# Weight preparation in three stages: load, square, and sum with scale, each a few steps apart

## The chip, the cores and the metric

The kernel runs on one core of one Trainium2 chip. The metric is the device time of the program in microseconds (us), measured in three runs. One further execution was profiled; all rows below come from it. The engines are TensorE (PE, matrix products; PEld is its weight load), VectorE (DVE), ScalarE (ACT), GpSimd (POOL) and SyncE (SP), which issues the loads.

## The reference

One decoder layer in float32 on 512 tokens of width 2048:

```python
hn = rms_norm(h, norm_mix)
h = h + nsa_mixer(hn, nsa_w_in, nsa_w_out, ...)      # sparse attention, 16 heads, 4 groups
hn = rms_norm(h, norm_ffn)
h = h + jnp.square(jax.nn.relu(hn @ ffn_w1)) @ ffn_w2    # F = 8192
gate = jax.nn.sigmoid(rms_norm(h, norm_ple) @ ple_w_gate)
h = h + (p @ ple_w_proj) * gate
return rms_norm(h, norm_final)
```

## The kernel before

The attention comes first (0 to about 870 us), then the MLP (to about 2110 us), then the gate stage. What follows speaks of the weights of the last two, since the change lies there.

**A weight's way.** A product in float32 accuracy is made of three matmuls on float16 halves: weight high x data high, weight high x data low, weight low x data high. So each weight goes through these steps, in pieces ("quarters") of 128 x 1024 float32, 512 KB:

1. *load* into one of six raw buffers (`raw`, RAWS = 6), issued by SP (L702);
2. *square*: ACT squares it and adds along each partition (`sum_sq`, L677; the squares themselves go to a PSUM bank and are not used, the trace calls them `s_ps`), which leaves one number per partition, `sq4`;
3. *sum*: PE adds these over the partitions with 128x1 matmuls against a tile of ones, `wb` (`scale_of`, the trace's `s_ps<-sq,wb`); a pair of weights has four such matmuls, a single one two;
4. *scale*: three small DVE operations make a power of two of the sum (L670 to L672);
5. *split*: ACT writes the scaled high half `wh` (L683), DVE the low half `wl` (L684), into one of nine slots (SLOTS = 9). The raw buffer is free once its last split is done.

**Items and the G loop.** The hidden width 8192 is worked in 16 groups G of four blocks. A group has `up` (h @ w1) and `down` (@ w2). From G = 2 on, `up` takes two "pair" items: two weight blocks of two quarters each, which `prepare` turns into seven slots, four of them with sums and differences of quarters (`S1`, `S2`, `s3`, `s4`, DVE adds at L725 to L731), for a scheme with seven products of 24 matmuls of 128x256 in place of eight. `down` takes four items of two quarters, 48 matmuls of 128x512 each. One G takes some 81 us, and the loop runs `down(G)`, then `up(G + 2)`.

**What orders the preparation.** `pump` (L751) does as much preparation as the buffers allow each time it is called: after every slot that is used up (`used`), and after three of the four steps `e` of a `down` item. At one call, in this order: scales of items that were staged at least LAG = 2 calls ago, loads and squares (`stage`) while raw buffers are free, splits while slots are free. At the attention's end `early` stages and scales the first five items one by one, with a lag of 0. The order in which a program's instructions then stand on each engine is settled by a scheduler that lists them by times of its own; each engine works strictly in that order.

Names that come up below: `x_ps` tiles are PSUM banks (`pt_ps` and `g_ps` hold products), `fh` and `fl` the halves of the hidden values, `xch` and `xcl` those of the MLP's input, `z` a copy of a product that is needed twice (L984), `ft` the hidden values before their square (L948), `fq` their sums of squares.

Of the kernel before, what the change touches and what calls it, by code (L numbers as in the profile page):

```python
# [9 lines left out]
BF16 = mybir.dt.bfloat16  # L10
# [16 lines left out]
NG = F // 128 // FG  # L27
NB = 32
HOLD = 9
LAG = 2  # L30
RAWS = 6
SLOTS = 9
STD = 2
# [8 lines left out]
def trunk_kernel(ctx, tc, xT, pT, gains, w_kcvc, w_blk, w_gates, w_out, w1c, w2c, posT,  # L42
# [21 lines left out]
    def sbank():  # L64
        return ps.tile([128, 2 * S], F32, name="s_ps", tag="s2", bufs=1)
# [18 lines left out]
    P = {}  # L84
# [23 lines left out]
    def wslice(hs, off, n=128):  # L108
# [31 lines left out]
                       fill=0.0, base=0, channel_multiplier=-1)  # L140
# [331 lines left out]
    def merge(gens, nfill, fill):  # L472
        n = [0] * len(gens)
        total = sum(c for _, c in gens)
        done = 0
        order = sorted((((j + 0.5) / c, gi) for gi, (_, c) in enumerate(gens) for j in range(c)))
        for x, (_, gi) in enumerate(order):
            next(gens[gi][0], None)
            want = int((x + 1) * nfill / total)
            while done < want:  # L480
                next(fill, None)
                done += 1
        for gg, _ in gens:
            drain(gg)
        while done < nfill:
            next(fill, None)
            done += 1

    with tc.tile_pool(name="st", bufs=2) as st:
# [3 lines left out]
        for c in range(2):  # L493
# [5 lines left out]
            for u in range(4):  # L499
                if c == 0:  # L500
                    n = 4 if u == 0 else 2
# [173 lines left out]
    def sum_sq(junk, src, sq):  # L675
        with nc.allow_low_precision(reason="a power of two is taken from it"):
            ACT.activation(junk, src, AF.Square, accum_out=sq)  # L677
# [15 lines left out]
    def stage(it):  # L693
        it.raw = []
        if len(it.src) == 2:
            quarters = [(it.src[a], b) for a, b in ((0, 0), (1, 0), (1, 1), (0, 1))]
        else:
            quarters = [(it.src[0], b) for b in range(need(it))]
        ps4 = P["sm"].tile([128, 4], BF16, name="sq4", tag="sq4")
        for x, (src, b) in enumerate(quarters):  # L700
            r = P["raw"].tile([128, 1024], F32, name="raw", tag="raw")
            nc.sync.dma_start(out=r, in_=src[:, b * 1024:(b + 1) * 1024])  # L702
            sum_sq(sbank()[:, 0:1024], r, ps4[:, x:x + 1])
            it.raw.append(r)
        it.sq = ps4[:, 0:len(quarters)]
        it.at = st["pumps"]

    def slot(it, name, src):
        hi = P["w16"].tile([128, 1024], F16, name="wh", tag="wh")
# [33 lines left out]
        if G > 0:  # L743
            items += [Item(ffn2[G - 1, c]) for c in range(4)]
    items += [Item(pT), Item(w_proj[1])] + [Item(w_pg[m]) for m in range(NK)]
    st = {"staged": 0, "split": 0, "gen": None, "raws": 0, "slots": 0, "limit": 0, "taken": 0, "scaled": 0, "pumps": 0}

    def need(it):
        return it.src[0].shape[-1] // 1024 * len(it.src)

    def pump(lag=LAG):  # L751
        st["pumps"] += 1
        while True:
            n = st["scaled"]
            if n < st["staged"] and st["pumps"] - items[n].at >= lag:
                items[n].sc, items[n].inv = scale_of(items[n].sq)
                st["scaled"] += 1
                continue
            n = st["staged"]
            if n < min(len(items), st["limit"]) and st["raws"] + need(items[n]) <= RAWS:  # L760
                stage(items[n])
                st["raws"] += need(items[n])
                st["staged"] += 1
                continue
            n = st["split"]
            if n < st["scaled"] and st["slots"] < SLOTS:
                if st["gen"] is None:
                    st["gen"] = prepare(items[n])
                    st["left"] = 7 if need(items[n]) == 4 else need(items[n])
                next(st["gen"])  # L770
                st["slots"] += 1
                st["left"] -= 1
                if need(items[n]) == 4:
                    st["raws"] -= {2: 2, 1: 1, 0: 1}.get(st["left"], 0)
                else:
                    st["raws"] -= 1
                if st["left"] == 0:
                    next(st["gen"], None)
                    st["gen"] = None
                    st["split"] += 1  # L780
                continue
            return
# [4 lines left out]

    def take():
        st["taken"] += 1
        return items[st["taken"] - 1]  # L790

    def early(n0, n1, gains=False):
        if gains:
            gain_scales()
            yield
        for n in range(n0, n1):
            st["limit"] = n + 1
            pump(0)
            yield

    def gain_scales():
# [16 lines left out]
    for hd in range(HEADS):  # L818
        n = counts[hd]
        pvg = pv_stage(hd, (pp, opool))  # L820
        if hd == 0:
            merge([(pvg, 10)], 16, fill)
            merge([(s_stage(1, (pp, small)), 5)], n - 16, fill)
        elif hd % HPG == 3 and hd + 1 < HEADS:
            merge([(pvg, 10)], 40, fill)
            merge([(s_stage(hd + 1, (pp, small)), 5)], n - 40, fill)
        elif hd + 2 < HEADS:
            merge([(pvg, 10), (s_stage(hd + 1, (pp, small)), 5)], n, fill)
        elif hd + 1 < HEADS:
            merge([(pvg, 10), (s_stage(hd + 1, (pp, small)), 5), (early(0, 2, True), 3)], n, fill)  # L830
        else:
            merge([(pvg, 10), (early(2, 4), 2)], n, fill)
        if hd == HEADS - 3:
            x_sb.close()
            for nm, bufs in (("sm", 12), ("keepc", 1), ("w16", SLOTS), ("raw", RAWS)):
                P[nm] = pool(nm, bufs)
        if hd == HEADS - 2:
            lo_eng[0] = DVE
    merge([(early(4, 5), 2)], 16, fill)
    drain(fill)  # L840
    a_sb.close()
    P["S"] = pool("S", 2, side="left")
# [66 lines left out]
    with ExitStack() as fx:  # L909
# [55 lines left out]
        def up_pair(G, j0, fq, ts, hook):  # L965
            it = take()
            ninv = P["sm"].tile([128, 1], F32, name="ninv", tag="ninv")
            DVE.tensor_scalar(ninv, it.inv, -1.0, None, op0=OP.mult)
            z = {}
            c = [wk.tile([128, S], F32, name="ft", tag="t") for _ in range(2)]  # L970
            o = {}

            def prod(b, w, x, first):
                if first:
                    o[b] = gbank()
                wh, wl = it.w[w]
                for k in range(8):
                    ws = slice(k * 128, (k + 1) * 128)
                    xh, xl = X[x, k]
                    mm3(o[b][:, 0:H2], wh[:, ws], wl[:, ws], xh, xl, first and k == 0, k == 7)  # L980

            def keep(n):
                z[n] = wk.tile([128, H2], F32, name="z", tag="z")
                ACT.activation(z[n], o["x"][:, 0:H2], AF.Copy)  # L984

            def total(e, half, n, b):
                DVE.tensor_add(c[e][:, half * H2:(half + 1) * H2], z[n], o[b][:, 0:H2])  # L987

            prod("x", "11", "11", True)
            keep(1)  # L990
            used()
            prod("v", "12", "21", True)
            total(0, 0, 1, "v")
            used()
            prod("x", "S2", "t2", False)
            keep(2)
            used()
            prod("y", "S1", "t1", True)
            used()
            hook(G, j0)  # L1000
            prod("x", "s3", "T3", False)
            keep(3)
            total(1, 1, 3, "y")
            used()
            prod("u", "22", "T4", True)
            total(1, 0, 3, "u")
            used()
            prod("y", "s4", "22", False)
            total(0, 1, 2, "y")
            used()  # L1010
            for e in (1, 0):
                DVE.tensor_scalar(c[e], c[e], ninv if e else it.inv, 0.0, op0=OP.mult, op1=OP.max)
            for e in range(2):
                squares(c[e], fq, j0 + e, ts)

        def up(G, prev=None):
            fq = P["sm"].tile([128, FG], F32, name="fq", tag="fq")
            ts = []

            def hook(G, j0):  # L1020
                if prev and j0 == 0:
                    sqd.append(squash(*prev))
                if G == 0 and j0 >= 2:
                    combos(j0 - 2)
                if G == 1 and j0 < 3:
                    combos(2 + 2 * j0)
                    combos(3 + 2 * j0)

            if G < STD:
                up_std(G, fq, ts, hook)  # L1030
            else:
                for j0 in (0, 2):
                    up_pair(G, j0, fq, ts, hook)
            return ts, fq

        def squash(ts, fq):
# [40 lines left out]
        for G in range(NG):  # L1077
            if G == NG - 1:
                st["limit"] = len(items) - NK + 2
            down(*sqd[G], G == NG - 1, made if G + 1 < NG else None)  # L1080
            if G + 2 < NG:
                made = up(G + 2)
# [154 lines left out]
```

## Time and profile before

| what | value |
|---|---|
| median of 3 runs | 2376.61 us (2374.44 to 2377.46) |
| profiled execution | 2376.99 us, span 2375.3 us |
| PE busy | 2315.4 us, 97% of the span |
| DVE, ACT, POOL busy | 1569.4, 1288.8 and 327.3 us |
| granted TensorE clock | 0.995 |
| moved by DMA | 232.52 MB, 98 GB/s in the mean |

The span reaches from the first to the last instruction; the execution's own time is 1.7 us longer. A matmul is drawn until its modelled end, which lies behind the start of the next, so the row of a wait shows less than what was lost; the times from start to start tell it.

### The profile page before, as it was taken

To read this page: it belongs to the slowest core of one execution; us is meant where nothing else is said; L and a number is where in the kernel's file an instruction comes from. 1 tells how busy PE (TensorE), PEld (TensorE's weight loads), DVE (VectorE), ACT (ScalarE), POOL (GpSimd) and SP (SyncE) were. 2 spreads that over 40 slices of the span, in tenths; PEclk is the share of its full clock that TensorE was granted. 3 is DMA by queue.
4 is the path that set the end of the run, shared out by engine and by line. 5 is a ranking of instruction groups with operands and counts; after the bars stand their busy time and mean duration, and the time that the engine had idled before them with its cause. 6 is when DMAs were issued, how large, how long until landed. Compare 5 with 4: busy or idle time off the path is not lost.

```text
span 2375.3 us, 35243 instructions
## 1 busy us (share of the span) xinstructions
PE 2315.4 (97%) x14042; PEld 1644.1 (69%) x14042; DVE 1569.4 (66%) x2737; ACT 1288.8 (54%) x2125; POOL 327.3 (14%) x176
## 2 busy tenths in 40 slices
PE   8999999999999999999999999999999999999997
PEld 6888888888888778567656665765576567654445
DVE  6347646656656968876776677667767776665742
ACT  5324434334333668576556656655665566565951
POOL 4253232333333120000000000000000000002012
PEclk9999999999999999999999999999999999999999
DMA  5231122122122413233223323332333233242411
GB/s 197 97 111 67 66 78 71 67 76 72 71 72 96 143 51 129 73 114 116 90 88 121 120 83 104 109 115 88 116 107 100 88 124 116 89 156 67 133 63 72
DMA packets 59062, 232.52 MB, mean 98 GB/s; under 512 B 6928, under 2 KB 7312, under 8 KB 51728
## 3 DMA queue, kind: packets, MB, share of 16 engines
q1 hardware_dynamic: 58896, 230.25, 28.9%
q8 instruction: 110, 1.80, 0.3%
q14 instruction: 56, 0.46, 0.1%
HBM read 223.94 MB, written 6.29 MB: 97 GB/s over the span
## 4 chain that ended last, share of the span: by engine, by line
PE 71%; DMA 10%; ACT 8%; DVE 6%; issue 4%; POOL 0%; SPq 0%; ACTq 0%; DVEq 0%; POOLq 0%
PE g_ps L71 42%; PE pt_ps L71 20%; DMA raw<-in_ffn_dram 9%; PE s_ps L71 5%; ACT wh L683 4%; ACT s_ps L677 3%; PE o_ps L71 3%; DVE wl L684 2%; PE pt_ps L427 1%; DVE ft L987 1%; DVE S L729 0%; DVE xt L881 0%; PE pt_ps L419 0%; DVE p L384 0%; DVE h L299 0%
## 5 line engine op out<-in xcount | busy, mean ns | idle before, releaser
L71 PEld LDWEIGHTS <-wh 128*128 128x128 f16 x6336 | 612.3, 98 | 353.0 <-issue 25.1
L684 DVE SCALAR_TENSOR_TENSOR wl<-raw,sc,wh 128x1024 f16<-128x1024 f32 x266 | 342.3, 1290 | 229.9 <-ACT wh L683 225.4
L71 PEld LDWEIGHTS <-wl 128*128 128x128 f16 x3168 | 309.7, 98 | 192.3 <-issue 24.7
L677 ACT ACTIVATE s_ps<-raw 128x1024 f32<-128x1024 f32 x294 | 301.1, 1024 | 239.8 <-DMA raw<-in_ffn_dram 206.5
L683 ACT ACTIVATE wh<-raw,sc 128x1024 f16<-128x1024 f32 x266 | 300.8, 1138 | 74.4 <-PE g_ps L71 61.2
L80 POOL TENSOR_TENSOR wl<-raw,wh 128x1024 fp32r<-128x1024 f32 x100 | 241.5, 2420 | 507.5 <-ACT wh L79 480.4
L179 POOL TENSOR_TENSOR ssacc<-ssacc,sq 128x512 f32<-128x512 f32 x50 | 71.3, 1427 | 1468.6 <-issue 1328.0
L79 ACT ACTIVATE wh<-raw 128x1024 fp32r<-128x1024 f32 (+1 forms) x122 | 125.6, 1044 | 225.0 <-PE g_ps L71 157.8
L71 PE MATMUL g_ps<-ah,wh 128*128 128x512 f32 x544 | 215.2, 396 | 0.0
L71 PE MATMUL g_ps<-ah,wl 128*128 128x512 f32 x544 | 214.1, 394 | 0.0
L71 PE MATMUL g_ps<-al,wh 128*128 128x512 f32 x544 | 212.7, 391 | 0.0
L71 PE MATMUL pt_ps<-fh,wh 128*128 128x512 f16 (+1 forms) x544 | 202.9, 373 | 3.5 <-ACT z L984 3.5
L71 PE MATMUL pt_ps<-fl,wh 128*128 128x512 f16 (+1 forms) x544 | 202.9, 373 | 0.0
L71 PE MATMUL pt_ps<-fh,wl 128*128 128x512 f16 (+1 forms) x544 | 202.9, 373 | 0.0
L71 PE MATMUL g_ps<-fh,wh 128*128 128x512 f16 (+1 forms) x544 | 202.8, 373 | 0.0
L71 PE MATMUL g_ps<-fh,wl 128*128 128x512 f16 (+1 forms) x544 | 202.7, 373 | 0.0
L71 PE MATMUL g_ps<-fl,wh 128*128 128x512 f16 (+1 forms) x544 | 202.7, 373 | 0.0
L684 DVE SCALAR_TENSOR_TENSOR wl<-S,sc,wh 128x1024 f16<-128x1024 f32 x112 | 143.5, 1281 | 88.0 <-ACT wh L683 88.0
L683 ACT ACTIVATE wh<-S,sc 128x1024 f16<-128x1024 f32 x112 | 128.0, 1142 | 69.9 <-PE pt_ps L71 42.1
L377 ACT ACTIVATE p<-s_ps,nm 128x128 f32<-128x128 f32 (+3 forms) x128 | 66.3, 524 | 113.9 <-DVE scm L373 57.3
L71 PE MATMUL pt_ps<-xcl,wh 128*128 128x256 f16 x448 | 122.1, 273 | 0.0
L71 PE MATMUL pt_ps<-xch,wh 128*128 128x256 f16 x448 | 122.1, 272 | 0.0
(286 smaller groups left out, 4897.4 us busy)
## 6 DMA issues: line engine op xcount, KB each, us to landing
raw<-in_ffn_dram SPq DMA_DIRECT2D x256, 512.0 KB, 3.9
raw<-in_w_blk_dram SPq DMA_DIRECT2D x32, 1024.0 KB, 4.8
raw<-in_w_out_dram SPq DMA_DIRECT2D x16, 1024.0 KB, 4.8
raw<-in_w_pg_dram SPq DMA_DIRECT2D x32, 512.0 KB, 3.9
h<-in_xT_dram SPq DMA_DIRECT2D x16, 256.0 KB, 6.5
raw<-in_w_kcvc_dram SPq DMA_DIRECT2D x4, 1024.0 KB, 4.7
raw<-in_w1c_dram SPq DMA_DIRECT2D x4, 1024.0 KB, 4.9
raw<-in_w_kcvc_dram SPq DMA_DIRECT2D x6, 512.0 KB, 5.8
```

Source lines behind the costliest of these rows:

```text
L71: nc.tensor.matmul(o, w, x, start=start, stop=stop, skip_group_check=True)
L79: ACT.activation(hi, src, AF.Copy)
L80: (eng or DVE).tensor_sub(lo, src, f32(hi))
L179: (DVE if e else POOL).tensor_add(acc[e], acc[e], sq)
L377: ACT.activation(p, v[:, b], AF.Exp, bias=nm[:, b:b + 1], accum_out=r[:, b:b + 1])
L427: nc.tensor.transpose(pt[:, (i - kc) * 128:(i - kc + 1) * 128], A["P", hd, b, i, kc], ident)
L677: ACT.activation(junk, src, AF.Square, accum_out=sq)
L683: ACT.activation(hi[:, cs], src[:, cs], AF.Copy, scale=sc)
L684: DVE.scalar_tensor_tensor(lo[:, cs], src[:, cs], sc, hi[:, cs], op0=OP.mult, op1=OP.subtract)
L987: DVE.tensor_add(c[e][:, half * H2:(half + 1) * H2], z[n], o[b][:, 0:H2])
```

## The change

Loading, squaring and the sum with the scale become three stages of `pump`. `stage` only issues the loads. A new `square` follows three calls later, the sum and scale five calls after the load (LAGS = (3, 5); before, the square was issued with the load and the scale two calls later). In the attention's tail `early` uses lags of 1 and 2 with more calls and a wider limit; from there to the end of the first `up`, and again from the last group on, the lags are 0 and 1. `take` issues what is still missing of an item that is about to be used.

```diff
-LAG = 2
+LAGS = (3, 5)
...
     def stage(it):
-        ps4 = P["sm"].tile([128, 4], BF16, name="sq4", tag="sq4")
-        for x, (src, b) in enumerate(quarters):
+        for src, b in quarters:
             r = P["raw"].tile([128, 1024], F32, name="raw", tag="raw")
             nc.sync.dma_start(out=r, in_=src[:, b * 1024:(b + 1) * 1024])
+            it.raw.append(r)
+        it.at = st["pumps"]
+
+    def square(it):
+        ps4 = P["sm"].tile([128, 4], BF16, name="sq4", tag="sq4")
+        for x, r in enumerate(it.raw):
             sum_sq(sbank()[:, 0:1024], r, ps4[:, x:x + 1])
-            it.raw.append(r)
-        it.sq = ps4[:, 0:len(quarters)]
-        it.at = st["pumps"]
+        it.sq = ps4[:, 0:len(it.raw)]
...
-    def pump(lag=LAG):
+    def pump(lags=None):
+        lags = lags or st["lags"]
         st["pumps"] += 1
         while True:
+            n = st["squared"]
+            if n < st["staged"] and st["pumps"] - items[n].at >= lags[0]:
+                square(items[n])
+                st["squared"] += 1
+                continue
             n = st["scaled"]
-            if n < st["staged"] and st["pumps"] - items[n].at >= lag:
+            if n < st["squared"] and st["pumps"] - items[n].at >= lags[1]:
                 items[n].sc, items[n].inv = scale_of(items[n].sq)
...
     def take():
         st["taken"] += 1
+        if st["scaled"] < st["taken"]:
+            pump((0, 0))
...
-        for n in range(n0, n1):
-            st["limit"] = n + 1
-            pump(0)
+        st["limit"] = n1
+        for n in range(n0):
+            pump((1, 2))
             yield
...
-            merge([(pvg, 10), (s_stage(hd + 1, (pp, small)), 5), (early(0, 2, True), 3)], n, fill)
+            merge([(pvg, 10), (s_stage(hd + 1, (pp, small)), 5), (early(4, 2, True), 5)], n, fill)
...
-            merge([(pvg, 10), (early(2, 4), 2)], n, fill)
+            merge([(pvg, 10), (early(4, 4), 4)], n, fill)
...
-    merge([(early(4, 5), 2)], 16, fill)
+    merge([(early(4, 5), 4)], 16, fill)
...
+            st["lags"] = LAGS
...
             if G == NG - 1:
                 st["limit"] = len(items) - NK + 2
+                st["lags"] = (0, 1)
```

The number of instructions of each kind is the same in both kernels. Where they stand is not. On PE, in the G period of the trace that begins near 1264 us, the first sum of the fourth ffn2 item stood in the kernel before like this (`sq4_12438` is that item's tile of sums; the second sum follows 24 matmuls later):

```order
L71 LDWEIGHTS wh_12218
L71 MATMUL pt_ps_12461<-xch_8778,wh_12218 128x256
L71 LDWEIGHTS wh_12218
L71 MATMUL pt_ps_12461<-xcl_8779,wh_12218 128x256
L71 LDWEIGHTS wb_93
L71 MATMUL s1_ps_12518<-sq4_12438,wb_93 128x1
L71 LDWEIGHTS wl_12219
L71 MATMUL pt_ps_12461<-xch_8778,wl_12219 128x256
```

In the changed kernel the same item's tile is `sq4_12535`, and both sums stand together:

```order
L71 LDWEIGHTS wh_12313
L71 MATMUL g_ps_12628<-xcl_8759,wh_12313 128x256
L71 LDWEIGHTS wl_12314
L71 MATMUL g_ps_12628<-xch_8758,wl_12314 128x256
L71 LDWEIGHTS wb_93
L71 MATMUL s1_ps_12616<-sq4_12535,wb_93 128x1
L71 LDWEIGHTS wb_93
L71 MATMUL s1_ps_12616<-sq4_12535,wb_93 128x1
L71 LDWEIGHTS wh_12313
L71 MATMUL g_ps_12628<-xch_8773,wh_12313 128x256
```

The first sum has moved back by 70 matmuls, the second by 47.

On ACT, the same place in the kernel before (`sq_12438` is the fourth ffn2 item again, `sq_12589` the next pair's first item, `ft_...` the hidden values):

```order
L984 ACTIVATE z<-pt_ps 128x256
L948 ACTIVATE ft_12453<-ft 128x512
L677 ACTIVATE s_ps,sq_12438<-raw 128x1024
L683 ACTIVATE wh<-raw,sc 128x1024
L948 ACTIVATE ft_12449<-ft 128x512
L677 ACTIVATE s_ps,sq_12438<-raw 128x1024
L683 ACTIVATE wh<-raw,sc 128x1024
L677 ACTIVATE s_ps,fq<-ft_12449 128x512
```

and in the changed kernel (`sq_12462` is the third ffn2 item, `sq_12535` the fourth, `sq_12683` the next pair's first item):

```order
L995 ACTIVATE z<-pt_ps 128x256
L959 ACTIVATE ft_12427<-ft 128x512
L683 ACTIVATE wh<-raw,sc 128x1024
L959 ACTIVATE ft_12423<-ft 128x512
L677 ACTIVATE s_ps,fq<-ft_12423 128x512
L683 ACTIVATE wh<-raw,sc 128x1024
L677 ACTIVATE s_ps,fq<-ft_12427 128x512
L677 ACTIVATE s_ps,sq_12462<-raw 128x1024
L995 ACTIVATE z<-pt_ps 128x256
L677 ACTIVATE s_ps,sq_12462<-raw 128x1024
L677 ACTIVATE s_ps,sq_12535<-raw 128x1024 x2
L677 ACTIVATE s_ps,sq_12683<-raw 128x1024
```

The squares of the third and fourth ffn2 item now stand behind the splits and the work on `ft`, and the squares of three items follow one another.

## Rows read from the trace of the kernel before

**Rows 1.** The page: span, PE's busy time, chain that ended last by line.
```profile
span 2375.3 us, 35243 instructions
...
PE 2315.4 (97%) x14042; PEld 1644.1 (69%) x14042; DVE 1569.4 (66%) x2737; ACT 1288.8 (54%) x2125; POOL 327.3 (14%) x176
...
PE g_ps L71 42%; PE pt_ps L71 20%; DMA raw<-in_ffn_dram 9%; PE s_ps L71 5%; ACT wh L683 4%; ACT s_ps L677 3%; PE o_ps L71 3%; DVE wl L684 2%; PE pt_ps L427 1%; DVE ft L987 1%; DVE S L729 0%; DVE xt L881 0%; PE pt_ps L419 0%; DVE p L384 0%; DVE h L299 0%
```

**Rows 2.** Waits of PE, whole run: releaser, us in total, times, longest.
```profile
PE s_ps L71 <- ACT s_ps L677: 24.9, 45, 1.4
```

**Rows 3.** Waits of PE, 960 to 2100 us.
```profile
PE s_ps L71 <- ACT s_ps L677: 22.1, 40, 1.4
PE pt_ps L71 <- ACT z L984: 3.5, 14, 0.3
```

**Rows 4.** Stretches: length; busy PE, PEld, DVE, ACT, POOL; clock, DMA, GB/s.
```profile
960.00:2100.00 1140.00, 1113.64 (x7650) 731.00 (x7649) 807.82 (x1283) 718.01 (x1066) 0.00 (x0) 1.00 0.32 105
1264.00:1345.00 81.00, 78.35 (x537) 51.05 (x536) 56.49 (x87) 51.34 (x76) 0.00 (x0) 1.00 0.32 102
```

**Rows 5.** Timeline of PE near 1264 us: start, length, instruction, idle before.
```profile
1264.27 0.27 PE L71 MATMUL pt_ps<-xch,wh 128*128 128x256 f16 x1
1264.38 0.27 PE L71 MATMUL pt_ps<-xcl,wh 128*128 128x256 f16 x1
1265.66 0.16 PE L71 MATMUL s_ps<-sq,wb 128*128 128x1 bf16 x1 [1.01 <-ACT s_ps L677]
```

**Rows 6.** Timeline of PE near 1277 us.
```profile
1276.98 0.38 PE L71 MATMUL pt_ps<-fh,wh 128*128 128x512 f16 x1
1277.20 0.38 PE L71 MATMUL pt_ps<-fl,wh 128*128 128x512 f16 x1
1278.37 0.16 PE L71 MATMUL s_ps<-sq,wb 128*128 128x1 bf16 x1 [0.79 <-ACT s_ps L677]
...
1279.68 0.38 PE L71 MATMUL pt_ps<-fh,wh 128*128 128x512 f16 x1 [0.26 <-ACT z L984]
```

**Rows 7.** Waits of ACT, 960 to 2100 us.
```profile
ACT s_ps L677 <- DMA raw<-in_ffn_dram: 196.1, 119, 3.9
```

**Rows 8.** Timeline of ACT, 1264 to 1280 us.
```profile
1264.46 1.03 ACT L677 ACTIVATE s_ps<-raw 128x1024 f32<-128x1024 f32 x1 [2.89 <-DMA raw<-in_ffn_dram]
1265.42 0.19 ACT L677 ACTIVATION_READ_ACCUMULATOR s_ps<-raw 128x1 bf16 x1
...
1277.17 1.03 ACT L677 ACTIVATE s_ps<-raw 128x1024 f32<-128x1024 f32 x1 [1.55 <-DMA raw<-in_ffn_dram]
...
1279.26 0.36 ACT L984 ACTIVATE z<-pt_ps 128x256 f32<-128x256 f32 x1
```

**Rows 9.** Waits of SP's loads, 960 to 2100 us.
```profile
SPq L702 <- DVE wl L684: 323.1, 81, 9.1
```

**Rows 10.** Line 702, the loads: time from issue to landing.
```profile
DMA to landing us min/median/max: 3.1/3.9/9.9
```

**Rows 11.** The page's groups: splits of raw pieces on DVE, ACT.
```profile
L684 DVE SCALAR_TENSOR_TENSOR wl<-raw,sc,wh 128x1024 f16<-128x1024 f32 x266 | 342.3, 1290 | 229.9 <-ACT wh L683 225.4
...
L683 ACT ACTIVATE wh<-raw,sc 128x1024 f16<-128x1024 f32 x266 | 300.8, 1138 | 74.4 <-PE g_ps L71 61.2
```

**Rows 12.** Timeline of DVE near 1271 us: scale operations, first and last.
```profile
1270.67 0.15 DVE L670 TENSOR_SCALAR e<-s_ps 128x1 int32<-128x1 int32 x1
...
1270.92 0.14 DVE L672 TENSOR_SCALAR sc<-e 128x1 int32<-128x1 int32 x1
```

**Rows 13.** Stretches of the attention's end and the gate stage.
```profile
780.00:870.00 90.00, 81.69 (x403) 61.07 (x402) 68.49 (x132) 55.26 (x99) 24.17 (x15) 0.98 0.30 100
2190.00:2300.00 110.00, 109.69 (x526) 49.71 (x526) 69.98 (x130) 82.69 (x125) 10.16 (x8) 0.98 0.32 106
```

More of the change, by code (lines that the diff above doesn't have):

```diff
@@ L745, in trunk_kernel @@
     items += [Item(pT), Item(w_proj[1])] + [Item(w_pg[m]) for m in range(NK)]
-    st = {"staged": 0, "split": 0, "gen": None, "raws": 0, "slots": 0, "limit": 0, "taken": 0, "scaled": 0, "pumps": 0}
+    st = {"staged": 0, "split": 0, "gen": None, "raws": 0, "slots": 0, "limit": 0, "taken": 0, "scaled": 0, "squared": 0, "pumps": 0, "lags": (0, 1)}
     def need(it):
         return it.src[0].shape[-1] // 1024 * len(it.src)
-    def pump(lag=LAG):
+    def pump(lags=None):
+        lags = lags or st["lags"]
         st["pumps"] += 1
         while True:
+            n = st["squared"]
[3 more added lines that the diff above has]
+                continue
             n = st["scaled"]
-            if n < st["staged"] and st["pumps"] - items[n].at >= lag:
+            if n < st["squared"] and st["pumps"] - items[n].at >= lags[1]:
                 items[n].sc, items[n].inv = scale_of(items[n].sq)
```

## The prediction, made before the changed kernel was run

> **What bounds the kernel now.** I read the page first: of a span of 2375.3 us TensorE (PE) is busy 2315.4, and the chain of work that ended last is PE in its two large lines, with a visible piece of "DMA raw", "ACT s_ps L677" and "PE s_ps" among them [rows 1]. So almost all of the time is matmul time, and what can be gained is the time in which PE stands. The list of waits by engine says for what PE stands: over the whole run one group leads by far, 45 waits of the sum over partitions (`s_ps`, the 128x1 matmuls of `scale_of`) for the square of a weight quarter on ScalarE (ACT, L677), 24.9 us [rows 2]. From 960 to 2100 us, the steady part of the MLP, only two groups are left: 40 of those 45, 22.1 us, and 14 waits for the copy `z` (L984), 3.5 us [rows 3]. No wait for a split weight is in the list. The table by stretches agrees: over 1140 us PE is busy 1113.6 at a granted clock of 1.00, and one G period of 81 us has 78.35 [rows 4].
>
> Next I looked at single waits. At 1264.38 a 128x256 matmul starts; the next start is due 0.11 us later, as between the rows above it, and is the sum at 1265.66. The loss is 1.17 us, of which the row shows 1.01: a matmul is drawn 0.16 us longer than the step to the next [rows 5]. For 128x512 it is the same (step 0.215, drawn 0.38, overhang 0.165) [rows 6]. So a wait costs its shown length plus about 0.16 us.
>
> On ACT the square that this sum wanted had itself waited 2.89 us for its load [rows 8]; in the MLP squares wait so 119 times, 196.1 us [rows 7]. And SP's loads wait for a raw buffer, which a split's second half (`wl`, L684) gives back [rows 9]. So the chain is: buffer free, load, square, sum; PE is at its end because the sum stands in PE's order soon after the load.
>
> **What the squares cost today.** Whole run: 24.9 + 45 x 0.16 = 32.1 us. `z`: 3.5 + 14 x 0.165 = 5.8 us. Together 37.9 us; in the MLP alone (22.1 + 40 x 0.16 + 5.8) / 14 = 2.45 us for each of 14 periods.
>
> **The change part by part.** Nothing is added or removed: the same loads, squares, sums, scale operations and splits are issued, in another order. Instruction durations stay as they are.
>
> 1. *Sums later on PE.* Adding the steps (0.11 and 0.215 us) of the matmuls that stand between old and new place, all sixteen quarters' sums of a period move back by 0.9 to 12 us: for the four items of ffn2 by 4.3 and 3.0, 12 and 9, 7.6 and 5.1, 3.3 and 1.7; for the two pairs by 2 to 6.5, and 0.9 for the last. The item in the first two listings of the change moves by 70 and 47 matmuls of 0.11. The longest wait of the run is 1.4 + 0.16 us [rows 3]. Where the square keeps its place, a sum that moves by more than that waits no more.
>
> 2. *Squares later on ACT.* ACT works in order, so a square that stands further back comes out later. In the third listing the squares of ffn2's last two items now stand behind one or two splits and the squares of `ft`. By the rows these are 1.14 us and 0.6 each [rows 11], say 3 to 4 us in all, against sums that moved 5 to 12. Most other squares keep their neighbours. What this gives: a square no longer stands waiting 2.89 us for its load with a split behind it that could run.
>
> 3. *Scales later.* The scale of an item now comes at the call in which its first split is issued, so for some items the split, and with it the giving back of the raw buffer and the next load, starts later. Prepared weights do not run out: PE has no wait for one now [rows 3], and counted through the calls the nine slots stay filled as before, but for one slot in two calls a period. The price is paid by the loads. The tightest place I found: after the second sum of ffn2's third item PE has 61 steps of 0.11 and 24 of 0.215, that is 12.0 us, until the last two sums of the next pair's first item. In this time must fit: sum 0.16; three scale operations 0.40 (1270.67 to 1271.06) [rows 12]; two `wh` with 1.04 from start to start and 1.14 for the last, 2.2; the last `wl` 1.28 [rows 11]; the load 3.9 [rows 10]; the square with its read-out, 1.03 and 0.19 less their overlap, 1.15 [rows 8]. Sum 9.1 us. On ACT `z` and two splits, 0.3 + 2 x 1.04 = 2.4, and the other quarter's square, 1.0, may come in between: 9.1 bare, 12.5 with all of them. I take 12.4, so 0.4 us of new wait a period, 14 x 0.4 = 5.6 us; bounds 0 (bare loop) and, with a load at the slowest landing of 9.9 [rows 10], 9.1 + 6.0 - 12.0 = 3.1 us a period, 43 us.
>
> 4. *`z`.* PE waits for it because ACT is on a split that began late, behind a square that waited for a load (1277.17, then z at 1279.26) [rows 6, 8]. The new order has two splits just ahead of `z`. I take half of the 5.8 us as gained, 2.9; bounds 0 and 5.8.
>
> 5. *The two ends.* In the attention's last part, 780 to 870 us, PE idles 8.3 of 90 us [rows 13], and the loads, squares and splits of the first items change places with the last softmax work. I know of no sign; taken as 0, bounds 4 us either way, half of the idle time. In the gate stage PE idles 0.3 of 110 us [rows 13]: at most 0.3 to gain, and 2 to lose where the first gate weights are split 1 to 1.5 us later.
>
> Sum against the profiled run, 2376.99 us (span and 1.7 around it): 2376.99 - 32.1 + 5.6 - 2.9 = 2347.6. The median of the runs is 2376.61, 0.4 less, so 2347.2; I say 2348.
>
> A rule of the Trainium skill speaks against this: Perfetto Trace Analysis, section "Optimization Strategy", says that the same gap repeating on the engine that should be saturated "can mean there isn't enough SBUF/PSUM for the next tile to be allocated". By it the remedy would be more raw buffers, and this change would give nothing, 2376. The rows bear out half: loads do wait for buffers, but 79 of 119 late squares already cost PE nothing.
>
> **The rivals.**
>
> *Half an effect (loads land later).* Loads now go out in closer bunches, with no square between. If those on the tight loop land halfway between median and slowest, (3.9 + 9.9) / 2 = 6.9 us, the loop is 12.1 bare, and 13.1 with the other quarter's square before it, 1.1 us over: 15.4 us lost, 2376.6 - 32.1 + 15.4 - 2.9 = 2357, and with `z` unchanged 2360. For it: landings do range from 3.1 to 9.9 [rows 10]. Against: DMA is 0.32 busy [rows 4]. DMA: Bandwidth & Descriptors in the Trainium skill, section "Issuing engines are not separate DMA queues", has transfers share 16 engines and interleave, which would favour this one; a landing far above the median in the tight loop would show it.
>
> *Nothing gained: the buffers set the pace.* Six raw buffers stay six. If squares come later exactly as the sums do, since the load behind each waits for the same split, PE meets them at the same distance: 2376. For it: 323.1 us of loads waiting for `wl` [rows 9]. Against: sums move up to 12 us within the period, and the load of an item is not issued later than before by the same count.
>
> *Slower: the longer loop.* Scale, split, buffer, load, square and sum stand in a ring, and the scale now comes later in it. From 12.0 + 2.45 = 14.5 us on, the new wait eats what is gained. With the slowest landing in each period the ring takes 15.1, 3.1 us over: 43 us against 32.1 + 2.9 gained, 2376.6 + 8 = 2385. For it: the slowest landing exists. Against: it would have to come in nearly every period, and the median is 3.9.
>
> **How the numbers follow.** The forecast (2340 to 2352) 0.62, the half effect 0.22, no gain 0.08, slower 0.08. A difference of 0.2%, 4.8 us, is about what a measurement of this kernel can tell from none. Forecast and half effect both lie below that: faster 0.84, same 0.08, slower 0.08. Lower end: all 37.9 us gained and 1.5 more in the attention, 2337. Upper end: the half effect with `z` unchanged and most of the 4 us lost in the attention's tail, and part of the way on to no gain, 2367.
>
> **What would show it.** Right: in the list of PE's waits the sums' group falls from 45 waits and 24.9 us to some 15 of about 0.3 us, all on the pair's last sums; PE's busy time in 960 to 2100 stays near 1114 us for the same work, in a stretch some 25 us shorter; ACT's waits for loads (196.1 us) shrink too. Half effect: waits of 1 us and more at the pair's last sums, behind loads that land in 6 to 7 us. No gain: some 40 waits again. Slower: waits of 3 us there, or a new group of PE waiting for `wh` or `wl`. The forecast is wrong if PE's waits fall as told and the time does not, since then a wait that the records draw as busy time has taken their place.

## The result, and the profile after

The changed kernel takes 2343.3 us in the median of 4 runs (2342.09 to 2345.7), the kernel before 2375.53 on the same occasion: a ratio of 0.9866, 95% interval 0.9849 to 0.9883, so 32 us less. The profiled execution took 2342.8 us, 34.2 less than the one of before.

The page of the changed kernel: span, busy time of the engines, the chain that ended last by engine.

```profile
span 2341.0 us, 35214 instructions
...
PE 2305.7 (98%) x14042; PEld 1644.0 (70%) x14042; DVE 1568.8 (67%) x2737; ACT 1286.5 (55%) x2125; POOL 326.6 (14%) x176
...
PE 91%; DVE 4%; ACT 2%; DMA 1%; issue 1%; POOL 0%; SPq 0%; DVEq 0%; ACTq 0%; POOLq 0%
```

PE now makes up 91% of the chain that ended last; ACT and DMA are nearly gone from it. In the kernel before the same line was:

```profile
PE 71%; DMA 10%; ACT 8%; DVE 6%; issue 4%; POOL 0%; SPq 0%; ACTq 0%; DVEq 0%; POOLq 0%
```

PE's busy time fell by 9.7 us although it does the same work. That is no faster matmul: the first 0.165 us of each wait is drawn as busy, under the overhang of the matmul before it. Of 45 and 14 waits [rows 2, 3] four are left; 55 fewer at 0.165 us are 9.1 us.

PE's waits over the whole run (releaser: us in total, times, longest), first the list's largest group and then what is left of [rows 2]:

```profile
PE o_ps L71 <- DVE tl L80: 4.7, 3, 1.9
...
PE s_ps L71 <- ACT s_ps L677: 1.0, 4, 0.4
```

From 960 to 2068 us the list of PE's waits is empty: the 40 waits for squares and the 14 for `z` of [rows 3] are all gone. ACT's waits for loads, and SP's for a split, 960 to 2070 us:

```profile
ACT s_ps L677 <- DMA raw<-in_ffn_dram: 96.9, 70, 3.6
```
```profile
SPq L701 <- DVE wl L684: 317.6, 96, 7.6
```

ACT waits half as long for loads as in [rows 7]; SP's loads wait for second halves of splits about as long as in [rows 9].

By stretches: PE's first MLP matmul (`x1h`) and first gate matmul (`xgh`), before and then after.

```profile
865.35 0.38 PE L71 MATMUL pt_ps<-x1h,wh 128*128 128x256 f16 x2 [1.29 <-ACT x1h L885]
...
2189.05 0.38 PE L71 MATMUL pt_ps<-xgh,wh 128*128 128x512 f16 x1 [1.50 <-ACT xgh L885]
```
```profile
869.53 0.40 PE L71 MATMUL pt_ps<-x1h,wh 128*128 128x256 f16 x2 [1.29 <-ACT x1h L896]
...
2154.16 0.38 PE L71 MATMUL pt_ps<-xgh,wh 128*128 128x512 f16 x1 [1.50 <-ACT xgh L896]
```

The attention ends 4.2 us later, the MLP (counted up to the first gate matmul) takes 1284.6 us instead of 1323.7, 39.1 less, and the rest 0.6 more: -34.3 us in the span.

### The profile page after: what moved, and what is told of

Its sections match the earlier page's. It is cut to its first block, busy times and chain, and to the rows that moved or that the text cites. A ratio compares the mean times of both kernels' runs of the same rounds, so it can differ in the third digit from the quotient of the medians.

```text
span 2341.0 us, 35214 instructions
## 1 busy us (share of the span) xinstructions
PE 2305.7 (98%) x14042; PEld 1644.0 (70%) x14042; DVE 1568.8 (67%) x2737; ACT 1286.5 (55%) x2125; POOL 326.6 (14%) x176
## 4 chain that ended last, share of the span: by engine, by line
PE 91%; DVE 4%; ACT 2%; DMA 1%; issue 1%; POOL 0%; SPq 0%; DVEq 0%; ACTq 0%; POOLq 0%
PE g_ps L71 50%; PE pt_ps L71 31%; PE s_ps L71 5%; PE o_ps L71 3%; PE pt_ps L427 1%; ACT s_ps L677 1%; DVE xt L892 1%; ACT wh L683 1%; DVE wl L684 1%; DMA h<-in_xT_dram 1%; DMA raw<-in_w_pg_dram 1%; DVE xgl L897 0%; PE pt_ps L419 0%; DVE h L299 0%; DVE p L384 0%
## 5 line engine op out<-in xcount | busy, mean ns | idle before, releaser
L377 ACT ACTIVATE p<-s_ps,nm 128x128 f32<-128x128 f32 (+3 forms) x128 | 66.4, 524 | 116.2 <-DVE scm L373 57.3
L71 PE MATMUL g_ps<-xch,wl 128*128 128x256 f16 x448 | 122.1, 272 | 0.0
```

The lines of the kernel that those rows point to most:

```text
L71: nc.tensor.matmul(o, w, x, start=start, stop=stop, skip_group_check=True)
L377: ACT.activation(p, v[:, b], AF.Exp, bias=nm[:, b:b + 1], accum_out=r[:, b:b + 1])
```

## The experiments

The two theories. *Distance*, the reason of my prediction: PE waits because its sums stand too soon behind the loads, and the later sums cure that. *ACT's queue*: ACT works in order, and a square whose load has not landed holds up the splits behind it; these would free the buffers for the next loads. Varied are the lags, the attention's tail and once the number of raw buffers; kernels that are compared in one paragraph ran on one chip, beside the kernel before, unless the text says otherwise.

### The sum alone later, and two references

```diff
-LAGS = (3, 5)
+LAGS = (0, 5)
```

This is sum_only; lag_0_3 has (0, 3) and undo_mlp (0, 2).

*sum_only.* 

> LAGS = (0, 5): the squares are issued with the loads again, as in the kernel before; only the sum and the scale come five calls later. Theory (distance): what PE loses is set by how much matmul work stands in PE's order between a load and its sum; the square's place does not matter. In PE's order the sums stand 1.6 to 8 us later than before (one 1.2 earlier), so the waits for squares in the MLP go: about 2343 us, within 4 of the changed kernel. Rival (ACT's queue): the gain comes from ACT no longer standing before a load that has not landed, with splits and z queued behind. Then ACT's waits for loads in the MLP are back near 196 us, PE waits for z 14 times again and for some squares: 2352 to 2362.

*lag_0_3.* 

> LAGS = (0, 3): squares with the loads, the sum one call later than before instead of three. The sums that wait in the kernel before (fourth ffn2 item, the next pair's first item) move by only -0.2 to 2.1 us in PE's order, the others by up to 2.6. Distance theory: most of the waits stay, some 25 to 40 in the MLP: 2360 to 2378. If it is enough that a stage of its own exists and loads go out in bunches, it would be near 2345.

*undo_mlp.* 

> LAGS = (0, 2): the MLP's lags as before; only the new tail of the attention (early with lags 1 and 2, more steps) and the lags of 0 and 1 at the start and the end are left. All sums of the MLP's periods stand where they stood in the kernel before. By the two traces the attention's end is 4.2 us longer in the changed kernel and the gate stage 0.6: if that is this part's doing, 2379 to 2382, slower than before by 0.1 to 0.25%. If the tail's price belongs to other runs' chance, 2375 to 2377.

Measured: the kernel before 2378.01 us (27 runs), sum_only 2381.24 (ratio 1.001, 0.9998 to 1.0023), lag_0_3 2383.35 (1.0021, 1.0012 to 1.003), undo_mlp 2384.86 (1.0027, 1.0015 to 1.0039). All three have the new tail, so undo_mlp is what the others compare with: a lag of five calls for the sum gained 3.6 us of some 40, and the intervals overlap. For sum_only both theories missed: it came out worse than even the rival had it. undo_mlp and lag_0_3 lie above their ranges too. In lag_0_3 the sums that waited have hardly moved, and there are still 40 waits, as the distance theory said; a square stage of its own, without a lag, gives nothing. The traces of sum_only and undo_mlp are of the slowest of their ten runs, so their times are not set against those of other kernels. Waits of PE, 960 to 2100 us, in undo_mlp and in sum_only:

```profile
PE s_ps L71 <- ACT s_ps L677: 27.2, 44, 2.2
PE pt_ps L71 <- ACT z L995: 3.1, 12, 0.3
```
```profile
PE s_ps L71 <- ACT s_ps L677: 16.3, 12, 2.8
PE pt_ps L71 <- ACT z L995: 12.6, 12, 2.6
```

The waits at sums fell from 44 to 12, but got longer, and `z` took over. All 12 are at one sum of each period, the last of the four of its second pair. This kernel moves it 1.2 us forward in PE's order, right behind the other three; the fifteen sums that moved back wait no more.

```profile
1230.38 0.22 PE L71 MATMUL s_ps<-sq,wb 128*128 128x1 bf16 x3
1231.77 0.16 PE L71 MATMUL s_ps<-sq,wb 128*128 128x1 bf16 x1 [1.17 <-ACT s_ps L677]
```

So sum_only is no clean test of the distance theory. With that sum in its old place some 12 x 1.2 = 14 of the 40 us might have been gained (an estimate); the longer waits for `z` are not touched by that. How they come about, ACT of sum_only near 1594 us shows:

```profile
1593.47 1.03 ACT L677 ACTIVATE s_ps<-raw 128x1024 f32<-128x1024 f32 x1 [2.85 <-DMA raw<-in_ffn_dram]
...
1597.83 1.03 ACT L677 ACTIVATE s_ps<-raw 128x1024 f32<-128x1024 f32 x1 [1.65 <-DMA raw<-in_ffn_dram]
1598.79 0.19 ACT L677 ACTIVATION_READ_ACCUMULATOR s_ps<-raw 128x1 bf16 x1
1598.88 1.13 ACT L683 ACTIVATE wh<-raw,sc 128x1024 f16<-128x1024 f32 x1
...
1600.54 0.36 ACT L995 ACTIVATE z<-pt_ps 128x256 f32<-128x256 f32 x1
```
```profile
1598.06 0.27 PE L71 MATMUL g_ps<-xch,wh 128*128 128x256 f16 x1
1600.95 0.27 PE L71 MATMUL pt_ps<-xch,wh 128*128 128x256 f16 x1 [2.62 <-ACT z L995]
```

ACT stands 2.85 and 1.65 us in front of squares, then works off the split and a square of `ft`, and PE loses 2.8 us waiting for a copy of 0.36 us that stood behind them. The square blocks, wherever the sum is.

A part of sum_only's time is the clock. In its trace the granted clock falls to 0.5 (1.2 GHz in place of 2.4) for 3.4 us after five of these waits, of 2.0 to 2.8 us; in the kernel before it does not between 870 and 2190 us. Each such stretch costs about 1.7 us (an estimate: half of 3.4). One of them, with the clock third from the end:

```profile
1315.40:1318.70 3.30, 3.30 (x10) 1.19 (x9) 1.91 (x3) 2.39 (x4) 0.00 (x0) 0.52 0.00 0
```

### The square later, the sum where it was

```diff
-LAGS = (3, 5)
+LAGS = (2, 2)
```

This is sq_2_sum_2; sq_3_sum_3 has (3, 3) and sq_3_sum_7 (3, 7). These and all that follow, but changed_again and in part tail_shares, have the attention's tail of before (its diff is with old_tail below).

*sq_2_sum_2.* 

> The attention's tail of before and LAGS = (2, 2): the sum and the scale keep the lag of two calls that they had in the kernel before, only the squares come two calls after the loads and right ahead of the sums. In PE's order 12 of 16 sums of a period stand where they stood or within 0.2 us, the fourth ffn2 item's 4.3 to 4.5 us later, the pair's by up to 1.1. Theory now (ACT's queue): PE loses its time where ACT stands in front of a square whose load has not landed, with z, the splits and so the next loads queued behind. The squares moved, so ACT's waits for loads in the MLP fall from 196 us to about 110 and the kernel comes close to the changed one with this tail: 2338 to 2350. Rival (distance of the sum in PE's order, my prediction's reason): sums that have not moved go on waiting, some 25 of 40 stay: 2358 to 2368.

*sq_3_sum_3.* 

> The attention's tail of before and LAGS = (3, 3): squares as in the changed kernel, sum and scale at the same call instead of two calls later. Queue theory: the squares' lag is what counts, 2337 to 2342, as with (3, 5). Distance theory: the first six sums of a period stand only 0 to 2.6 us later than before instead of 0.9 to 5.2, so a few waits come back there: 2342 to 2352. A third of both would be that PE, with the sum right behind the square, meets squares that ACT has not reached: then some 14 to 28 short waits.

*sq_3_sum_7.* 

> The attention's tail of before and LAGS = (3, 7): the scale two calls later still; sums 4 to 17.5 us later than in the kernel before. The ring (sum, scale, split, buffer free, load, square, sum) gets longer and prepared weights come later. If the ring has slack, 2336 to 2340 as with (3, 5). If it is the price of a late scale, as the prediction's slower rival has it, PE waits for wh or wl or for squares again, 1 us and more in every period: 2350 to 2400. I lean to the second.

Measured, against 2371.9 us of the kernel before on this chip: 2339.78 (0.9864, 0.9848 to 0.9881), 2339.1 (0.986, 0.9846 to 0.9875) and 2338.84 (0.9859, 0.9845 to 0.9874). All the gain is there with the sum's lag untouched, and whether the sum follows at once or four calls later makes no difference; two calls later, run on other chips (old_tail below), it took 2337.56 and 2338.51 us. PE's waits in sq_2_sum_2, 960 to 2070 us:

```profile
PE pt_ps L71 <- ACT z L995: 1.1, 2, 0.8
PE s_ps L71 <- ACT s_ps L677: 0.3, 1, 0.3
```

In sq_3_sum_3 and sq_3_sum_7 that list is empty. So the distance theory falls as the reason of the gain, and with (3, 7) also my fear of the longer ring, to which I had leaned: sums up to 17.5 us later cost nothing that these runs show.

### Two squares of sixteen

The diff is against the kernel of old_tail.

```diff
-LAGS = (3, 5)
+LAGS = (0, 2)
...
             self.src = src
+            self.late = 0
...
             items += [Item(ffn2[G - 1, c]) for c in range(4)]
+            items[-1].late = 2
...
-            if n < st["staged"] and st["pumps"] - items[n].at >= lags[0]:
+            if n < st["staged"] and st["pumps"] - items[n].at >= max(lags[0], items[n].late if lags[1] > 1 else 0):
```

*late_fourth_only.* 

> The attention's tail of before, LAGS = (0, 2) as in the kernel before, and one exception: the fourth ffn2 item of every group is squared two calls after its load, all other squares come with the loads. In ACT's order two of sixteen squares a period move back, behind two splits and the work on ft; in PE's order the fourth item's sums move by 4.5 and 4.3 us, the others by 1.1 at most. Queue theory: these two squares stood in front of the splits that free the buffers for the next pair's loads; moving them alone gives nearly all of it, 2337 to 2345, and the sums of the next pair, which have not moved, stop waiting. If it takes the other squares' later place too: 2350 to 2365.

Measured: 2342.16 us (0.9859, 0.9846 to 0.9873) against 2376.49 of the kernel before. On the same chip the whole change with this tail takes 2338.51; so one item's two squares a group bring 34.3 of 38.0 us. PE's waits, 960 to 2070 us:

```profile
PE pt_ps L71 <- ACT z L997: 1.2, 4, 0.7
```

The place itself, ACT and SP's loads, in the kernel before (the squares between are the first of [rows 8] and its fellow) and then here:

```profile
1260.94 0.63 ACT L948 ACTIVATE ft<-ft 128x512 f32<-128x512 f32 x1
...
1265.51 1.13 ACT L683 ACTIVATE wh<-raw,sc 128x1024 f16<-128x1024 f32 x1
...
1268.30 1.13 ACT L683 ACTIVATE wh<-raw,sc 128x1024 f16<-128x1024 f32 x1
```
```profile
1267.99 0.33 SPq L702 DMA_DIRECT2D raw<-in_ffn_dram  x1
...
1270.78 0.33 SPq L702 DMA_DIRECT2D raw<-in_ffn_dram  x1
```
```profile
1252.39 0.63 ACT L961 ACTIVATE ft<-ft 128x512 f32<-128x512 f32 x1
1253.78 1.15 ACT L683 ACTIVATE wh<-raw,sc 128x1024 f16<-128x1024 f32 x1 [0.76 <-PE g_ps L71]
...
1255.40 1.13 ACT L683 ACTIVATE wh<-raw,sc 128x1024 f16<-128x1024 f32 x1
```
```profile
1256.28 0.33 SPq L702 DMA_DIRECT2D raw<-in_ffn_dram  x1
...
1257.88 0.33 SPq L702 DMA_DIRECT2D raw<-in_ffn_dram  x1
```

Reckoned from the start of `ft`, the two splits came 4.6 and 7.4 us later and the two loads behind them 7.1 and 9.8; now 1.4 and 3.0, and 3.9 and 5.5. The loads are those of the next pair's quarters. They go out 3.2 and 4.3 us sooner, and the pair's sums, which stand where they stood to within 1.1 us, find their squares done. This shows the whole path: late load, blocked ACT, late split, buffer late, next load late.

The 1.1 us alone do not explain it. 25 of the 40 waits of before stood at the second and third of these sums. Counted from the last sum of the third ffn2 item, which has not moved, their two squares were done after 13.4 and 16.0 us and now after 11.0 and 13.6 (medians of the periods from 960 us on); PE comes to the sums after 13.2 and 14.7 us, and with the old squares it would still have waited, at the second of the two more than 1 us. Another 14 of the 40 waits stood at the fourth item's own sums. Those must follow their squares, 4.5 us back; what the later place of the sum does there by itself these runs do not tell.

### Fewer buffers

```diff
-RAWS = 6
+RAWS = 5
```

*raws_5.* 

> The attention's tail of before, LAGS = (3, 5) and five raw buffers instead of six. Nothing else is changed, but with fewer free buffers loads are issued later, and the sums stand 8 to 22 us later in PE's order than in the kernel before. If six buffers set the pace (the prediction's rival 'nothing gained'), one fewer costs at once: PE waits of several us in each period, 2400 and more. If the order on ACT was the bound and buffers have slack, 2337 to 2350.

Measured, with LAGS = (3, 5): 2342.32 us (0.9878, 0.9863 to 0.9892), some 3 us above the other three on this chip. Even with five buffers it beats the kernel before with six by 29.6 us. More than six were not tried.

### The attention's tail

```diff
-        st["limit"] = n1
-        for n in range(n0):
-            pump((1, 2))
+        for n in range(n0, n1):
+            st["limit"] = n + 1
+            pump((0, 0))
...
-            merge([(pvg, 10), (s_stage(hd + 1, (pp, small)), 5), (early(4, 2, True), 5)], n, fill)
+            merge([(pvg, 10), (s_stage(hd + 1, (pp, small)), 5), (early(0, 2, True), 3)], n, fill)
...
-            merge([(pvg, 10), (early(4, 4), 4)], n, fill)
+            merge([(pvg, 10), (early(2, 4), 2)], n, fill)
...
-    merge([(early(4, 5), 4)], 16, fill)
+    merge([(early(4, 5), 2)], 16, fill)
```

The new shares 5, 4 and 4 in place of 3, 2 and 2 make tail_shares of old_tail.

*old_tail.* 

> The changed kernel with the attention's tail of before: early stages and scales one item a step with lags of 0, with the old shares of the merge. MLP as in the changed kernel. If the new tail costs its 4.2 us, this one takes 2338 to 2340, about 0.18% less than the changed kernel; PE's waits for tl near 790 to 830 us are then back to 2.1 us from 4.7. If the tail is not the cause, 2342 to 2344.

*changed_again, old_tail_again and tail_shares, on one chip.* 

> The changed kernel once more, on the same chip as the two that follow: a ratio of 0.985 to 0.988 to the kernel before.

 

> The changed kernel's MLP with the attention's tail of before, on the same chip: 4 to 6 us less than the changed kernel if the new tail costs what the runs so far say; equal to it if that came from the chip.

 

> As the one before, early staging and scaling one item a step with lags of 0, but with the shares of the merge from the changed kernel (5, 4 and 4 instead of 3, 2 and 2). In PE's order the last head's scores then stand 18 rows later than in the kernel before; in the changed kernel it is 26. If the shares' shift of the last head's scores is the tail's cost, most of the 4 to 6 us is back. If it is the squares and splits in the tail, it is as fast as the one before.

Measured: old_tail 2337.56 us (0.9828, 0.9813 to 0.9842). On one chip, before 2376.49: changed_again 2343.83 (0.9864, 0.9851 to 0.9878), old_tail_again 2338.51 (0.9845, 0.9832 to 0.9859), tail_shares 2340.15 (0.9849, 0.9836 to 0.9863). So the new tail costs about 5 us (undo_mlp, from the other side, has 6.9), and old_tail beats both kernels. By the medians the shares alone are 1.6 us of it, little beside the scatter of the runs. The start of the last head's softmax on ACT (an Exp, L377, of 128x512), before and after, shows where the cost begins:

```profile
795.22 0.69 ACT L377 ACTIVATE p<-s_ps,nm 128x512 f32<-128x512 f32 x1 [0.24 <-DVE nm L371]
```
```profile
800.17 0.69 ACT L377 ACTIVATE p<-s_ps,nm 128x512 f32<-128x512 f32 x1 [2.57 <-DVE sc L671]
```

It comes 5.0 us later, and PE then waits 4.7 us for `tl` in place of 2.1 with the old tail. The traces give the shares more than the medians do: this Exp follows that of the head before by 9.0 us in the kernel before and in old_tail_again, by 12.6 in tail_shares and by 13.7 in the changed kernel, and PE's waits from 780 to 872 us sum to 7.8 us in old_tail_again, 10.3 in tail_shares and 10.3 in changed_again. What the changed kernel has beyond tail_shares is the clock. Behind two waits of 0.89 and 1.79 us, the second until 828.56, the granted clock (third from the end) is 0.50, 1.2 GHz:

```profile
828.80:832.20 3.40, 3.40 (x14) 2.30 (x14) 0.00 (x0) 0.60 (x1) 0.00 (x0) 0.50 0.77 265
```

That costs some 1.7 us (an estimate, half of 3.4). Such a stretch between 780 and 860 us is in all five traces with the new tail and in none of the nine others. Which of the moved instructions makes the waits, the weights' squares and splits on ACT and DVE or the scores' later place on PE, was not tried one by one and stays open.

## Why the prediction was right, and where not

- **The time** (2348 forecast, 2343.3 measured, inside 2337 to 2367) and the place, PE's waits for squares, were right. All 32.1 us of them but 1.6 us went.
- **Part 1, sums later on PE, was the wrong reason.** I gave it the gain: "a sum that moves by more than that waits no more". In sum_only that held for the fifteen sums that moved back, and yet next to nothing was gained: PE waited for `z` and for the one sum that moved forward. sq_2_sum_2 leaves 12 of 16 within half a us of their place and gains all. I took the square's time as given and moved only the sum that waits for it, but the square's time is set by its load, and the load's by a split that ACT reaches late. Two readings there are off, without weight: the third ffn2 item's sums move by 11.0 and 8.0 us in the trace, not 12 and 9, and the 0.6 us of a square of `ft` in part 2 is not in [rows 11], though other rows of the trace have it (0.58 to 0.60).
- **Part 2, squares later on ACT, was the right reason, priced at nothing.** I counted it as a delay of squares by 3 to 4 us, and only noted that a split could then run. That remark was the mechanism. So the good number is in part luck: this kernel moves sums and squares together, and what I gave to the one came from the other.
- **Part 3: 5.6 us for the longer ring, measured 0.** Against PE's 12.0 us of work I had put a ring of 12.4. In the changed kernel, from the third ffn2 item's last sum to the end of the pair's fourth square, it takes 11.0 us near 1264 us and 10.6 to 11.4 in the other periods, so PE finds the square done:

```profile
1264.57 0.17 PE L71 MATMUL s_ps<-sq,wb 128*128 128x1 bf16 x1
1276.53 0.19 PE L71 MATMUL s_ps<-sq,wb 128*128 128x1 bf16 x2
```
```profile
1275.38 0.19 ACT L677 ACTIVATION_READ_ACCUMULATOR s_ps<-raw 128x1 bf16 x1
```

The 15 short waits that I had expected there did not come.
- **Part 4: half of `z`'s 5.8 us, measured all.** It was the same blocking.
- **Not counted: 2.6 us** in waits too short to be listed. By the starts of PE's matmuls, 24 steps were 0.1 to 0.3 us too long in the MLP, 3.8 us together; now 11, 1.2 us. Ten of each are no waits, but matmuls at a granted clock of 0.5 at the MLP's start.
- **Part 5: the tail, taken as 0 with bounds of 4, cost 4.2 us** in the trace and about 5 in the runs, more than its bound. Of the 4.2 us PE's waits are 2.3 (10.4 against 8.1 from 780 to 872 us) and the clock some 1.7; I had no term for either. Gate stage 0.6, within its bound.

The terms on the profiled runs: 39.1 gained in the MLP and 4.8 lost outside, 34.3 against 29.4 forecast. The errors, 5.6 + 2.9 + 2.6 - 1.6 - 4.2 - 0.6 = 4.7, make up the difference of 4.9 to within 0.2.

- **The rivals.** *Loads land later*: the median is 3.9 us as before and the slowest 10.0.

```profile
DMA to landing us min/median/max: 3.1/3.9/10.0
```

DMA: Bandwidth & Descriptors in the Trainium skill, section "Issuing engines are not separate DMA queues", says that transfers interleave on the same 16 engines. No price of that shows here, at a DMA share of 0.32 [rows 4]. *The buffers set the pace*: raws_5 speaks against it. Perfetto Trace Analysis in the Trainium skill, section "Optimization Strategy", says that a repeating gap "can mean there isn't enough SBUF/PSUM". That was not its cause here: the gap that came back in every group was closed with the same buffers, and stayed closed with one fewer. The rows that seemed to bear it out, loads waiting for a split [rows 9], are about the same (317.6 us) in the kernel without the gap. *The longer loop*: not seen, nor at (3, 7).

## What to carry to other kernels

When an engine with an in-order queue waits for a transfer, ask what stands behind the waiting instruction, above all what would free the buffer for the next transfer. Move the instruction that waits, not the one that waits for it; it may take one place in the queue of many. Before giving a gain to one of several edits that come together, try each alone: here the later sum by itself brought 3.6 of some 40 us, and the new tail cost 5.

## What was not expected

ACT's waiting time as such says little: in late_fourth_only it still waits 148.2 us for loads in 960 to 2070 us, and PE for none of their squares.

```profile
ACT s_ps L677 <- DMA raw<-in_ffn_dram: 148.2, 86, 4.8
```

What counts is which two of these squares stand ahead of a split that is due. And PE's waits are not all in the rows that are called so: 0.165 us of each is drawn as busy (9.1 us), and the shortest are not listed at all (2.6), together some 12 of the 39 us. Nor do the rows of waits show what a wait costs behind its end: where the granted clock fell after it, another 1.7 us (the estimate above).
